# One transformer layer on one core: where two norm weights and the attention gates are multiplied in

## The chip, the cores and the metric

The kernel runs on one core of a Trainium2 chip. The metric is device time in microseconds for one execution; lower is better. The kernel before takes 1735.78 us, the median of three runs (1735.76 to 1736.35).

The engines are named as the profile names them: PE is TensorE (matrix products; PEld are its weight loads), DVE is VectorE, ACT is ScalarE, POOL is GpSimd, and SP is the engine whose queue issues the DMAs. A line number such as L207 is a line of the kernel before.

## The reference, cut to what matters

```python
def rms_norm(x, g):
    xf = x.astype(jnp.float32)
    y = xf * lax.rsqrt(jnp.mean(xf * xf, axis=-1, keepdims=True) + RMS_EPS)
    return (y * g.astype(jnp.float32)).astype(x.dtype)

def hybrid_layer(x, mem, norm_mix, w_in, ...):
    xn = rms_norm(x, norm_mix)              # 1024 rows of 1024 channels
    proj = xn @ w_in                        # q, k, v, gates, conv input, memory q, merge gates
    ...
    kvm = rms_norm(mem, norm_mem) @ w_mem_kv   # 256 rows of 1024 channels
    ...
    # nsa_attention, for each of three branches (compressed, selected, window):
    #   p = masked_softmax(s, mask); o = p @ v
    return gg[..., 0:1] * o_c + gg[..., 1:2] * o_s + gg[..., 2:3] * o_w
```

The rows of x and mem are divided by their root mean square and multiplied by one weight per channel. In the attention each head's probabilities are divided by their row sum, and each branch is multiplied by a sigmoid gate, one per row, head and branch.

## The kernel before

Products are made with operands split into a high part (rounded to a TensorE format) and a low part (the rest): `split(hi, lo, src)` is a copy on ACT (L131) and a subtraction on DVE (L128), and a product is three matmuls, all recorded at L144.

**Start.** x is read in four pairs of 128-row tiles (`rows2`, L229). For each pair `norm_x` calls `norm_pair`: for each of the two tiles a Square with a running sum on ACT (L205), a square root on ACT (L136), a reciprocal on DVE (L138), and a DVE operation (L207) that multiplies the tile by the row factor and by `gmix`, the norm weights spread over all 128 partitions, into a work slab. `gmix` is made by two products of a column of ones with the weight row (L324) and two DVE operations (L325). Then `transpose_pair` turns the pair with 16 PE transposes (L216) into four PSUM banks of 128 x 2 x 256, and each bank is split into a slab of `XN`. The first projection (memory queries, `raw_proj`, 48 matmuls of 128x256 per pair) follows each pair, and the convolution's input products follow that.

**Memory.** `norm_pair` also serves mem; its weights come in by a DMA that spreads them over the partitions (`gain_row`, L197).

**Attention.** Units (query tile, group, branch, head pair) run four ahead of their value products. `scores` makes the scores on PE, a masked minimum on DVE (L707, L679), the exponential with its sum on ACT (L711, L681), and ends in `softmax_tail`: a reciprocal of the sums (L645), a product with the gates into `c` (L651), both on DVE, and one POOL operation per head that multiplies the probabilities by `c` (L653). POOL also makes `qd`, the next query tile's queries times their norm weight (L661), which PE turns at L665.

**Order.** A scheduler sets each engine's order from the written program and its pools of buffers; an engine then runs its list in order. Products of the merge gates (`pf` banks, `fsl` weights) are written with a lower priority as filler, so that they stand wherever other PE work is not ready; from the thirteenth on their weights' subtraction is on POOL (L128).

Of the kernel before, what the change touches and what calls it, by code (L numbers as in the profile page):

```python
# [8 lines left out]
F32 = mybir.dt.float32  # L9
F32R = mybir.dt.float32r  # L10
BF16 = mybir.dt.bfloat16
# [6 lines left out]
P = 128  # L18
# [21 lines left out]
def hybrid_layer_kernel(  # L40
# [154 lines left out]
    def gain_row(src):  # L195
        g = t4([D])
        nc.sync.dma_start(g, src.to_broadcast([P, D]))  # L197
        return g

    def norm_pair(src, gain, dests, js):  # L200

        for tt in range(2):
            j = js[tt]
            ss = small(1)
            nc.scalar.activation(j, src[:, tt, :], AF.Square, accum_out=ss)  # L205
            r = recip_rms(ss, D, RMS_EPS, 1)
            nc.vector.scalar_tensor_tensor(j, src[:, tt, :], r, gain, op0=OP.mult, op1=OP.mult)  # L207
        transpose_pair(js, dests)

    def transpose_pair(js, dests):  # L210
        for kp in range(4):
            b = bank([2, 256])
            for kk in range(2):
                k = 2 * kp + kk
                for tt in range(2):
                    nc.tensor.transpose(b[:, kk, tt * P:(tt + 1) * P], js[tt][:, k * P:(k + 1) * P], ident)  # L216
            hi, lo = dests(kp)
            split(hi, lo, b)
# [13 lines left out]
    def work2():  # L232
        js = slab([2, D], F32)
        return js[:, 0, :], js[:, 1, :]

    def norm_x(tp):
        half, q = tp // 2, tp % 2
        js = work2()
        if q == 0:
            for kp in range(4):  # L240
                XN[half][kp] = slab([2, 2, 512])
        norm_pair(xin[tp], gmix, lambda kp: tuple(XN[half][kp][:, hl, :, q * 256:(q + 1) * 256] for hl in range(2)),
                  js)
# [73 lines left out]
    xin = [rows2(x, 0)]  # L317
    g1 = [t2([512], p=1) for _ in range(2)]
    for half in range(2):
        nc.sync.dma_start(g1[half], norm_mix[:, half * 512:(half + 1) * 512])  # L320
    gmix = t4([D])
    for half in range(2):
        b = bank([512])
        nc.tensor.matmul(b, ones[0:1, :], g1[half], start=True, stop=True)  # L324
        nc.vector.tensor_scalar(gmix[:, half * 512:(half + 1) * 512], b, 512.0, None, op0=OP.mult)  # L325
# [138 lines left out]
    gme = gain_row(norm_mem)  # L464
    js = work2()
    MN = [slab([2, 4, 256]) for _ in range(2)]
    norm_pair(xs, gme, lambda kp: tuple(MN[kp // 2][:, hl, 2 * (kp % 2):2 * (kp % 2) + 2, :] for hl in range(2)), js)
# [174 lines left out]
    def softmax_tail(i, g, br, h0, den, tiles):  # L642
        n = len(tiles)
        rec, c = small(n), small(n)
        nc.vector.reciprocal(rec, den)  # L645
        c0 = (4 * g + h0) * 3 + br
        gate = gsb[:, i, c0:c0 + 3 * n - 2:3]
        if br == 0 and i == 0:
            nc.vector.scalar_tensor_tensor(c, rec, rowok, gate, op0=OP.mult, op1=OP.mult)
        else:  # L650
            nc.vector.tensor_tensor(c, rec, gate, op=OP.mult)  # L651
        for h in range(n):
            nc.gpsimd.tensor_scalar(tiles[h], tiles[h], c[:, h:h + 1], 1.0, op0=OP.mult, op1=OP.mult)  # L653
# [225 lines left out]
    def norm_h(tp):  # L879
# [14 lines left out]
        def turned(kp):  # L894
            b = bank([2, 256])
            for kk in range(2):
                k = 2 * kp + kk
                for tt in range(2):
                    nc.tensor.transpose(b[:, kk, tt * P:(tt + 1) * P], js[tt][:, k * P:(k + 1) * P], ident)
            split(XN[half][kp][:, 0, :, c], XN[half][kp][:, 1, :, c], b)  # L900
            return b
# [274 lines left out]
```

## Time and profile before

| what | us |
|---|---|
| median of three runs | 1735.78 |
| the profiled execution | 1737.04 |
| its span, first to last instruction | 1735.3 |
| PE busy in the span | 1704.0 |
| DVE busy | 1087.8 |
| ACT busy | 732.3 |
| POOL busy | 482.8 |

The rows further down are of four kinds. The page gives each engine's busy time. Tables by stretch give busy time in a window of the span, with the granted TensorE clock as a share of its full 2.4 GHz. Timelines list instructions in order of time; square brackets give the idle time just before and what ended it. Groups by form give count, busy time and mean duration of one kind of instruction.

### The profile page before, as it was taken

The numbers are of one execution on the slowest core, as the hardware profiler recorded it, in microseconds if no ns is written. First come the engines' busy times: TensorE is split into PE (matmuls) and PEld (weight loads), VectorE is DVE, ScalarE is ACT, GpSimd is POOL, SyncE is SP. The second block draws the span as 40 slices with busy tenths as digits, with TensorE's granted clock in tenths as the row PEclk, the third lists the DMA queues.
The fourth block names the chain that finished last, engine by engine and source line by source line (L and its number), as shares of the span: only waits on it lengthen the run. The fifth ranks groups of instructions, "written<-read, shape, count | busy, mean of one in ns | idle before, by whom it ended". The sixth has DMA issues, their size and how long they took to land. (4 is left out here: it accounts for less than half of the span.)

```text
span 1735.3 us, 25240 instructions
## 1 busy us (share of the span) xinstructions
PE 1704.0 (98%) x9483; PEld 1480.1 (85%) x9483; DVE 1087.8 (63%) x1885; ACT 732.3 (42%) x1378; POOL 482.8 (28%) x469
## 2 busy tenths in 40 slices
PE   6999999999999999999999999999999999999999
PEld 5887998999888889989888899788888888888887
DVE  5499897877345667777754624865544545457665
ACT  5211443344356666666653423632232322234332
POOL 0000001110134443444204500165556677410000
PEclk9999999999999999999999999999999999999999
DMA  6112442122111111111385322143233445794673
GB/s 203 47 38 97 135 121 90 39 73 74 49 61 56 56 49 34 31 46 50 106 306 183 109 80 98 73 134 98 91 122 97 158 149 167 256 388 153 223 240 122
DMA packets 178388, 204.08 MB, mean 118 GB/s; under 512 B 10774, under 2 KB 125750, under 8 KB 177242
## 3 DMA queue, kind: packets, MB, share of 16 engines
q1 hardware_dynamic: 178266, 202.47, 35.5%
q8 instruction: 74, 1.21, 0.3%
q14 instruction: 48, 0.39, 0.1%
HBM read 152.10 MB, written 50.33 MB: 117 GB/s over the span
## 5 line engine op out<-in xcount | busy, mean ns | idle before, releaser
L144 PE MATMUL ps<-slab,wsl 128*128 128x512 f32 (+1 forms) x1664 | 371.8, 382 | 3.0 <-DVE t L128 2.4
L144 PEld LDWEIGHTS ps<-slab,wsl 128*128 128x128 f32 x1664 | 303.1, 189 | 64.2 <-issue 2.6
L144 PE MATMUL pf<-slab,fsl 128*128 128x512 f32 x1236 | 321.5, 399 | 1.2 <-ACT fz L791 1.1
L144 PEld LDWEIGHTS pf<-slab,fsl 128*128 128x128 f32 x1236 | 223.3, 189 | 42.2 <-ACT fz L791 2.3
L144 PE MATMUL ps<-wsl,slab 128*128 128x256 f32 x1680 | 217.3, 285 | 0.0
L144 PEld LDWEIGHTS ps<-wsl,slab 128*128 128x128 f32 x1680 | 209.1, 193 | 2.0 <-issue 0.7
L1006 DVE TENSOR_TENSOR t<-ps,t 128x512 f32<-128x512 f32 x127 | 86.9, 688 | 113.9 <-PE ps L144 111.0
L365 DVE SCALAR_TENSOR_TENSOR slab<-slab,cw 128x1023 f32<-128x1023 f32 (+15 forms) x120 | 151.4, 1266 | 1.8
L144 PE MATMUL ps<-slab,fsl 128*128 128x512 f32 x636 | 147.7, 389 | 0.0
L144 PEld LDWEIGHTS ps<-slab,fsl 128*128 128x128 f32 x636 | 119.4, 188 | 24.8
L128 DVE TENSOR_TENSOR t<-ps,t 128x512 fp32r<-128x512 f32 (+3 forms) x196 | 120.3, 630 | 15.5 <-ACT t L131 14.0
L1110 PE MATMUL ps<-wsl 128*128 128x512 f32 x495 | 118.5, 389 | 0.0
L128 DVE TENSOR_TENSOR wsl<-st,wsl 128x1024 fp32r<-128x1024 f32 x65 | 84.7, 1303 | 53.5 <-ACT wsl L131 50.4
L144 PE MATMUL ps<-t,slab 128*128 128x256 f32 x624 | 115.5, 293 | 1.6 <-DVE t L128 1.0
L131 ACT CAST t<-ps 128x512 fp32r<-128x512 f32 (+2 forms) x192 | 98.0, 539 | 36.4 <-PE ps L739 25.4
L1110 PEld LDWEIGHTS ps<-wsl 128*128 128x128 f32 x495 | 92.9, 188 | 19.3
L131 ACT CAST wsl<-st 128x1024 fp32r<-128x1024 f32 x65 | 68.3, 1051 | 84.7 <-PE ps L144 45.4
L521 POOL TENSOR_SCALAR t<-t,sm 128x256 f32<-128x256 f32 x32 | 22.5, 722 | 288.1 <-DVE sm L517 288.1
L144 PEld LDWEIGHTS ps<-t,slab 128*128 128x128 f32 x624 | 94.9, 191 | 7.8 <-DVE t L128 1.7
L144 PE MATMUL ps<-slab,qt 128*128 128x384 f32 (+3 forms) x384 | 96.1, 342 | 1.9 <-DVE sm L707 1.9
L131 ACT CAST wsl<-t 128x1024 fp32r<-128x1024 f32 x42 | 44.3, 1054 | 97.8 <-POOL t L128 38.9
L1110 PE MATMUL ps<-fsl 128*128 128x512 f32 x330 | 79.8, 389 | 0.0
(233 smaller groups left out, 2693.6 us busy)
## 6 DMA issues: line engine op xcount, KB each, us to landing
t<-in_w_down_dram SPq DMA_DIRECT2D x70, 256.0 KB, 4.3
fst<-in_w_in_dram SPq DMA_DIRECT2D x24, 512.0 KB, 3.8
zd<-fz SPq DMA_DIRECT2D x48, 256.0 KB, 2.0
t<-zd SPq DMA_DIRECT2D x24, 512.0 KB, 4.1
st<-in_w_in_dram SPq DMA_DIRECT2D x22, 512.0 KB, 4.0
st<-in_w_gate_dram SPq DMA_DIRECT2D x22, 512.0 KB, 4.3
st<-in_w_up_dram SPq DMA_DIRECT2D x22, 512.0 KB, 4.1
ad<-t SPq DMA_DIRECT2D x44, 256.0 KB, 2.4
```

The source lines that it names most:

```text
L128: eng.tensor_tensor(o, a, b, op=OP.subtract)
L131: nc.scalar.copy(hi, src)
L144: m = nc.tensor.matmul(o, a, b, start=start, stop=stop)
L365: return nc.vector.scalar_tensor_tensor(acc[:, s:], u[:, :S - s], cw[:, ct, 30 - s:31 - s], acc[:, s:], op0=OP.mult, op1=OP.add)
L521: nc.gpsimd.tensor_scalar(pm[:, tt, h, :], pm[:, tt, h, :], rec[:, j:j + 1], 1.0, op0=OP.mult, op1=OP.mult)
L1006: nc.vector.tensor_tensor(o, a_, b_, op=OP.add)
L1110: nc.tensor.matmul(B[t], a_, b_, start=start and k == 0 and j == 0, stop=k == FH - 1 and j == 2, skip_group_check=True)
```

## The change

`gain_row`, `work2` and the weight products are gone. The weights of both norms come in as 16 rows of 128 numbers, are turned once on PE, and stay as `gcol`, a tile of 128 x 16 with one weight per partition. `norm_pair` scales the rows in place with the row factor alone (a DVE operation with one scalar), and turns them from there. After the turn a channel lies on a partition, so the weight is applied in the split: per bank two ACT copies of 128x256 with a scale from `gcol` and two DVE operations of 128x256, where one of each on 128x512 stood. The second tile of the first pair is read after the weight rows. The Square writes to a small BF16 tile.

In `softmax_tail` the product `c` is gone: POOL multiplies by the reciprocal and by the gate at once. In the first query tile's compressed branch a DVE operation multiplies the reciprocal by `rowok`.

```diff
-    def norm_pair(src, gain, dests, js):
+    gcol = const([2 * KT], F32, "gcol")
+    def norm_pair(src, g0, dests):
         for tt in range(2):
-            j = js[tt]
+            v = src[:, tt, :]
             ss = small(1)
-            nc.scalar.activation(j, src[:, tt, :], AF.Square, accum_out=ss)
+            nc.scalar.activation(t2([D], BF16), v, AF.Square, accum_out=ss)
             r = recip_rms(ss, D, RMS_EPS, 1)
-            nc.vector.scalar_tensor_tensor(j, src[:, tt, :], r, gain, op0=OP.mult, op1=OP.mult)
-        transpose_pair(js, dests)
+            nc.vector.tensor_scalar(v, v, r, None, op0=OP.mult)
+        for kp in range(4):
+            b = turned_pair([src[:, tt, :] for tt in range(2)], kp)
+            hi, lo = dests(kp)
+            for kk in range(2):
+                g = gcol[:, g0 + 2 * kp + kk:g0 + 2 * kp + kk + 1]
+                nc.scalar.activation(hi[:, kk], b[:, kk], AF.Copy, scale=g)
+                nc.vector.scalar_tensor_tensor(lo[:, kk], b[:, kk], g, hi[:, kk].bitcast(F32), op0=OP.mult,
+                                               op1=OP.subtract)
...
-    xin = [rows2(x, 0)]
-    g1 = [t2([512], p=1) for _ in range(2)]
-    for half in range(2):
-        nc.sync.dma_start(g1[half], norm_mix[:, half * 512:(half + 1) * 512])
-    gmix = t4([D])
-    for half in range(2):
-        b = bank([512])
-        nc.tensor.matmul(b, ones[0:1, :], g1[half], start=True, stop=True)
-        nc.vector.tensor_scalar(gmix[:, half * 512:(half + 1) * 512], b, 512.0, None, op0=OP.mult)
+    xin = [slab([2, D], F32)]
+    nc.sync.dma_start(xin[0][:, 0, :], x[:P, :])
+    rows = t2([P], p=2 * KT)
+    nc.sync.dma_start(rows[:KT, :], norm_mix.rearrange("o (k p) -> (o k) p", p=P))
+    nc.sync.dma_start(rows[KT:, :], norm_mem.rearrange("o (k p) -> (o k) p", p=P))
+    nc.sync.dma_start(xin[0][:, 1, :], x[P:2 * P, :])
+    b = bank([2 * KT])
+    nc.tensor.transpose(b, rows, ident[:2 * KT, :2 * KT])
+    nc.vector.tensor_copy(gcol, b)
...
     def softmax_tail(i, g, br, h0, den, tiles):
         n = len(tiles)
-        rec, c = small(n), small(n)
+        rec = small(n)
         nc.vector.reciprocal(rec, den)
-        c0 = (4 * g + h0) * 3 + br
-        gate = gsb[:, i, c0:c0 + 3 * n - 2:3]
         if br == 0 and i == 0:
-            nc.vector.scalar_tensor_tensor(c, rec, rowok, gate, op0=OP.mult, op1=OP.mult)
-        else:
-            nc.vector.tensor_tensor(c, rec, gate, op=OP.mult)
+            nc.vector.tensor_scalar(rec, rec, rowok, None, op0=OP.mult)
         for h in range(n):
-            nc.gpsimd.tensor_scalar(tiles[h], tiles[h], c[:, h:h + 1], 1.0, op0=OP.mult, op1=OP.mult)
+            c0 = (4 * g + h0 + h) * 3 + br
+            nc.gpsimd.tensor_scalar(tiles[h], tiles[h], rec[:, h:h + 1], gsb[:, i, c0:c0 + 1], op0=OP.mult, op1=OP.mult)
```

ACT at the start, before: after the first tile's Square (L205) come the casts of the first two weight units (`st` to `wsl`), and the first pair's four banks are split before the second pair's Square.

```order
L205 ACTIVATE slab_173,sm_178<-slab_139 128x1024
L131 CAST wsl_155<-st_153 128x1024
L136 ACTIVATE sm_180<-sm_178 128x1
L131 CAST wsl_160<-st_158 128x1024
L205 ACTIVATE slab_173,sm_185<-slab_139 128x1024
L136 ACTIVATE sm_187<-sm_185 128x1
L131 CAST slab_174<-ps_192 128x2x256
L131 CAST slab_175<-ps_199 128x2x256
L131 CAST slab_176<-ps_206 128x2x256
L131 CAST slab_177<-ps_213 128x2x256
L205 ACTIVATE slab_220,sm_221<-slab_163 128x1024
L136 ACTIVATE sm_223<-sm_221 128x1
```

ACT at the start, now (its lines are those of the changed kernel: L203 the Square, L136 the root, L211 the scaled copy of half a bank; `slab_140` is the first pair of x, `slab_159` the second):

```order
L203 ACTIVATE t_17_174,sm_173<-slab_140 128x1024
L136 ACTIVATE sm_176<-sm_173 128x1
L203 ACTIVATE t_21_182,sm_181<-slab_140 128x1024
L136 ACTIVATE sm_184<-sm_181 128x1
L131 CAST wsl_151<-st_149 128x1024
L131 CAST wsl_156<-st_154 128x1024
L211 ACTIVATE slab_169<-ps_189,gcol 128x256
L211 ACTIVATE slab_170<-ps_198,gcol 128x256
L203 ACTIVATE t_29_226,sm_225<-slab_159 128x1024
L211 ACTIVATE slab_171<-ps_207,gcol 128x256
L211 ACTIVATE slab_172<-ps_216,gcol 128x256
L136 ACTIVATE sm_228<-sm_225 128x1
```

Both Squares and roots of the first pair now stand ahead of the weight casts, and the second pair's Square stands between the first pair's half-bank copies.

DVE at the start, before, from the first weight unit's subtraction on (`slab_174` to `slab_177` are the first pair's split slabs):

```order
L128 TENSOR_TENSOR wsl_155<-st_153,wsl_155 128x1024
L138 RECIPROCAL sm_182<-sm_180 128x1
L325 TENSOR_SCALAR t_5_146<-ps_150 128x512
L128 TENSOR_TENSOR wsl_160<-st_158,wsl_160 128x1024
L207 SCALAR_TENSOR_TENSOR slab_173<-slab_139,sm_182,t_5_146 128x1024
L138 RECIPROCAL sm_189<-sm_187 128x1
L207 SCALAR_TENSOR_TENSOR slab_173<-slab_139,sm_189,t_5_146 128x1024
L128 TENSOR_TENSOR slab_174<-ps_192,slab_174 128x2x256
```

DVE at the start, now (L205 is the scaling in place, L212 the low half of a bank):

```order
L138 RECIPROCAL sm_186<-sm_184 128x1
L205 TENSOR_SCALAR slab_140<-slab_140,sm_186 128x1024
L128 TENSOR_TENSOR wsl_151<-st_149,wsl_151 128x1024
L128 TENSOR_TENSOR wsl_156<-st_154,wsl_156 128x1024
L212 SCALAR_TENSOR_TENSOR slab_169<-ps_189,gcol,slab_169 128x256
L212 SCALAR_TENSOR_TENSOR slab_170<-ps_198,gcol,slab_170 128x256
L212 SCALAR_TENSOR_TENSOR slab_171<-ps_207,gcol,slab_171 128x256
L212 SCALAR_TENSOR_TENSOR slab_172<-ps_216,gcol,slab_172 128x256
L138 RECIPROCAL sm_230<-sm_228 128x1
L212 SCALAR_TENSOR_TENSOR slab_169<-ps_189,gcol,slab_169 128x256
L205 TENSOR_SCALAR slab_159<-slab_159,sm_230 128x1024
```

The scaling of the first pair has moved ahead of the weight subtractions, and the second pair's first scaling stands among the first pair's half banks. On PE nothing moves at this place: the 16 transposes of the first pair and four of the second still stand ahead of the first projection matmul.

DVE in the attention, fifth query tile, before (`sm_5357` is `c`; L707 is the masked minimum of the next unit):

```order
L645 RECIPROCAL sm_5356<-sm_5337 128x2
L651 TENSOR_TENSOR sm_5357<-sm_5356,gsb 128x2
L707 ISA wsl_5392,sm_5393<-ps_5395,strip 128x384
L707 ISA sm_5393 128x1
L128 TENSOR_TENSOR t_963_5457<-ps_5456,t_963_5457 128x512
```

DVE at the same place, now (L640 is the reciprocal, L699 the masked minimum):

```order
L640 RECIPROCAL sm_5313<-sm_5294 128x2
L699 ISA wsl_5347,sm_5348<-ps_5350,strip 128x384
L699 ISA sm_5348 128x1
L128 TENSOR_TENSOR t_919_5408<-ps_5407,t_919_5408 128x512
L699 ISA wsl_5347,sm_5348<-ps_5354,strip,sm_5348 128x256
```

The product with the gates is gone from between the reciprocal and the next masked minimum.

## Rows read from the trace of the kernel before

**Rows 1.** The page, busy time of each engine and share of span.

```profile
PE 1704.0 (98%) x9483; PEld 1480.1 (85%) x9483; DVE 1087.8 (63%) x1885; ACT 732.3 (42%) x1378; POOL 482.8 (28%) x469
```

**Rows 2.** By stretch: length, busy PE, PEld, DVE, ACT, POOL; clock; DMA share, GB/s.

```profile
0.00:30.00 30.00, 16.50 (x83) 13.14 (x84) 16.87 (x24) 15.91 (x27) 3.13 (x13) 0.94 0.85 275
30.00:60.00 30.00, 28.60 (x212) 26.94 (x212) 14.64 (x23) 13.83 (x29) 0.26 (x2) 1.00 0.10 30
...
600.00:700.00 100.00, 97.79 (x618) 88.29 (x619) 67.78 (x228) 62.38 (x151) 40.09 (x53) 0.98 0.13 40
...
1200.00:1300.00 100.00, 100.00 (x443) 82.81 (x442) 49.11 (x57) 28.69 (x37) 56.80 (x38) 1.00 0.35 111
```

**Rows 3.** Timeline of the start: start us, us, engine, line, instruction, idle before.

```profile
4.46 1.06 ACT L205 ACTIVATE slab<-slab 128x1024 f32<-128x1024 f32 x1 [2.17 <-DMA slab<-in_x_dram]
...
8.12 1.04 ACT L131 CAST wsl<-st 128x1024 fp32r<-128x1024 f32 x1 [2.50 <-DMA st<-in_w_in_dram]
...
9.53 1.04 ACT L131 CAST wsl<-st 128x1024 fp32r<-128x1024 f32 x1 [0.27 <-DMA st<-in_w_in_dram]
...
11.00 1.22 DVE L128 TENSOR_TENSOR wsl<-st,wsl 128x1024 fp32r<-128x1024 f32 x1
...
12.13 1.28 DVE L207 SCALAR_TENSOR_TENSOR slab<-slab,sm,t 128x1024 f32<-128x1024 f32 x1
...
15.80 2.51 ACT L131 CAST slab<-ps 128x512 fp32r<-128x512 f32 x4 [3.93 <-PE ps L216]
16.41 2.61 DVE L128 TENSOR_TENSOR slab<-ps,slab 128x512 fp32r<-128x512 f32 x4 [1.61 <-ACT slab L131]
18.20 1.06 ACT L205 ACTIVATE slab<-slab 128x1024 f32<-128x1024 f32 x1
...
19.49 1.04 ACT L205 ACTIVATE slab<-slab 128x1024 f32<-128x1024 f32 x1
...
21.16 1.12 PE L216 MATMUL ps<-ident,slab 128*128 128x128 f32 x4 [3.48 <-DVE slab L207]
...
21.92 4.82 PE L144 MATMUL ps<-wsl,slab 128*128 128x256 f32 x29
...
44.71 0.63 PE L216 MATMUL ps<-ident,slab 128*128 128x128 f32 x4 [1.40 <-DVE slab L207]
```

**Rows 4.** PE alone by stretch of 2 us: length, busy PE, granted clock, DMA share.

```profile
22.00:24.00 2.00, 2.00 (x12) 0.50 0.40 102
...
650.00:652.00 2.00, 2.00 (x8) 0.50 0.00 0
```

**Rows 5.** Groups by form: count, busy us, mean ns of one, idle before.

```profile
L128 DVE TENSOR_TENSOR t<-ps,t 128x256 fp32r<-128x256 f32 x40 | 16.4, 417 | 1.2 <-ACT t L131 1.1
...
L364 DVE TENSOR_SCALAR slab<-slab,cw 128x1024 f32<-128x1024 f32 x4 | 3.2, 809 | 0.0
...
L515 ACT ACTIVATE t<-ps,sm 128x256 f32<-128x256 f32 x32 | 14.8, 473 | 31.9 <-DVE sm L511 31.8
...
L131 ACT CAST slab<-ps 128x256 fp32r<-128x256 f32 x8 | 3.0, 370 | 5.8 <-DVE t L290 5.8
```

**Rows 6.** Timeline of the attention around 645 us.

```profile
641.73 2.41 POOL L128 TENSOR_TENSOR fsl<-fst,fsl 128x1024 fp32r<-128x1024 f32 x1 [2.67 <-ACT fsl L131]
...
642.77 1.38 DVE L651 TENSOR_TENSOR sm<-sm,gsb 128x2 f32<-128x2 f32 x1
...
647.64 0.50 PE L144 MATMUL ps<-slab,qt 128*128 128x256 f32 x2 [1.34 <-DVE sm L707]
```

**Rows 7.** Groups by form in the attention.

```profile
L651 DVE TENSOR_TENSOR sm<-sm,gsb 128x2 f32<-128x2 f32 x64 | 20.7, 323 | 5.6
...
L661 POOL TENSOR_TENSOR t<-slab,gn 128x512 f32<-128x512 f32 x16 | 20.7, 1296 | 88.0 <-DVE sm L287 88.0
...
L653 POOL TENSOR_SCALAR wsl<-wsl,sm 128x512 f32<-128x512 f32 x12 | 8.2, 695 | 6.1 <-DVE sm L651 5.9
```

**Rows 8.** PE's waits in the span: us in total, times, longest.

```profile
PE ps L665 <- POOL t L661: 1.8, 2, 0.9
```

More of the change, by code (lines that the diff above doesn't have):

```diff
@@ L193, in hybrid_layer_kernel, with turned_pair @@
     md = drp.tile([4, P, S], F32, tag="md", name="md")
[L195 to L198, printed above, removed]
-    def norm_pair(src, gain, dests, js):
+    gcol = const([2 * KT], F32, "gcol")
+    def norm_pair(src, g0, dests):
         for tt in range(2):
-            j = js[tt]
+            v = src[:, tt, :]
             ss = small(1)
-            nc.scalar.activation(j, src[:, tt, :], AF.Square, accum_out=ss)
+            nc.scalar.activation(t2([D], BF16), v, AF.Square, accum_out=ss)
             r = recip_rms(ss, D, RMS_EPS, 1)
-            nc.vector.scalar_tensor_tensor(j, src[:, tt, :], r, gain, op0=OP.mult, op1=OP.mult)
-        transpose_pair(js, dests)
-    def transpose_pair(js, dests):
+            nc.vector.tensor_scalar(v, v, r, None, op0=OP.mult)
         for kp in range(4):
-            b = bank([2, 256])
+            b = turned_pair([src[:, tt, :] for tt in range(2)], kp)
+            hi, lo = dests(kp)
             for kk in range(2):
[L214 to L218, printed above, removed]
+                g = gcol[:, g0 + 2 * kp + kk:g0 + 2 * kp + kk + 1]
+                nc.scalar.activation(hi[:, kk], b[:, kk], AF.Copy, scale=g)
+                nc.vector.scalar_tensor_tensor(lo[:, kk], b[:, kk], g, hi[:, kk].bitcast(F32), op0=OP.mult,
+                                               op1=OP.subtract)
+    def turned_pair(js, kp):
+        b = bank([2, 256])
+        for kk in range(2):
+            k = 2 * kp + kk
+            for tt in range(2):
+                nc.tensor.transpose(b[:, kk, tt * P:(tt + 1) * P], js[tt][:, k * P:(k + 1) * P], ident)
+        return b
     XN = [[None] * 4 for _ in range(2)]
@@ L230, in rows2 @@
         return xs
-    def work2():
-        js = slab([2, D], F32)
-        return js[:, 0, :], js[:, 1, :]
     def norm_x(tp):
         half, q = tp // 2, tp % 2
-        js = work2()
         if q == 0:
@@ L241, in norm_x @@
                 XN[half][kp] = slab([2, 2, 512])
-        norm_pair(xin[tp], gmix, lambda kp: tuple(XN[half][kp][:, hl, :, q * 256:(q + 1) * 256] for hl in range(2)),
-                  js)
+        norm_pair(xin[tp], 0, lambda kp: tuple(XN[half][kp][:, hl, :, q * 256:(q + 1) * 256] for hl in range(2)))
     def unit(src, shape, alloc=wslab, eng=None, load=False):
@@ L463, in hybrid_layer_kernel @@
     xs = rows2(mem, 0)
-    gme = gain_row(norm_mem)
-    js = work2()
     MN = [slab([2, 4, 256]) for _ in range(2)]
-    norm_pair(xs, gme, lambda kp: tuple(MN[kp // 2][:, hl, 2 * (kp % 2):2 * (kp % 2) + 2, :] for hl in range(2)), js)
+    norm_pair(xs, KT, lambda kp: tuple(MN[kp // 2][:, hl, 2 * (kp % 2):2 * (kp % 2) + 2, :] for hl in range(2)))
     def mn(hl, k, half, a, b):
@@ L894, in turned @@
         def turned(kp):
[L895 to L899, printed above, removed]
+            b = turned_pair(js, kp)
             split(XN[half][kp][:, 0, :, c], XN[half][kp][:, 1, :, c], b)
```

## The prediction

> **What bounds the kernel now.** I read the page first. PE is busy for 1704.0 of 1735.3 us [rows 1], so only 31 us of the span can be won by work that isn't PE's, and the question for every part of the change is whether it touches one of the places where PE stands. The table by stretch finds them [rows 2]: 13.5 us of PE's idle time lie in the first 30 us and 1.4 us in the next 30; 2.2 us lie between 600 and 700, where the attention runs; between 1200 and 1300 PE has no idle time at all. DVE, ACT and POOL are below 70% in the attention stretch, so work taken from them there is worth nothing by itself, only through a wait of PE that it shortens.
>
> The timeline of the start [rows 3] is to be read as one chain. The first tile of x is there at 4.46. ACT squares it, and then waits for a weight unit: the cast at 8.12 stands ahead of the root in its list, idle 2.50 us for the DMA, and the second cast at 9.53 is again set by a DMA. So the root comes at 9, the scalings L207 run from 12.13, the splits on ACT end at 18.3 and on DVE at 19.0, and only behind them ACT takes the second pair's Squares (18.20 and 19.49). PE's first four transposes of the second pair (21.16, idle 3.48 us for L207) stand ahead of the first projection matmul, so real work begins at 21.92, with the clock at 0.50, that is 1.2 GHz, right after this idle time [rows 4].
>
> **The change at the start.** Three edits act on this chain. The Squares and roots of the first pair go ahead of the weight casts; the wait for `gmix` goes; the second pair's first Square goes between the first pair's half banks. Against them stands a dearer split. I walk the new lists with durations of the old trace.
>
> Prices. A half-bank copy on ACT with a scale from `gcol`: the plain 128x256 copy takes 0.37 us, and one of the same size with a per-partition operand (L515, an exponential) 0.47 [rows 5]; I take 0.47, since that operand is what is added, and keep 0.37 as the lower end. A half-bank low part on DVE: 0.42 for 128x256 from PSUM [rows 5], and L207, which has such an operand, takes 0.06 more than L128 of the same size (1.28 against 1.22) [rows 3]; I take 0.48, with ends 0.42 and 0.60. The scaling in place: L364 is the same kind of operation on the same size and takes 0.81 [rows 5]. A Square with its read takes 1.15, with the root 1.29, the step from 18.20 to 19.49 [rows 3].
>
> Walk. The first tile at 4.46 is squared, rooted and scaled by about 7; the second tile, issued two small DMAs later, lies between 4.46 and the next arrival at 8.12, so its scaling ends near 9 and at the latest near 10.5. The 16 transposes then end before or near 12. ACT is held by the second weight cast, which ends at 9.53 + 1.04 = 10.57 whatever else moves. From there its list is two halves (to 11.5), the Square of the second pair (to 12.7), two halves (13.1, 13.6), a root (13.8), and then the second halves (14.3, 14.7). DVE ends the second weight subtraction at 10.6 + 1.22 = 11.85, does two halves (12.8), two more as ACT delivers them (13.7, 14.2), a reciprocal (14.4), one half (14.9), and then the scaling of the second pair's first tile, which ends at 15.7. Now PE has its four transposes, at 15.75 where the old ones began at 21.16. The gain at that point is 5.4 us; with the cheaper prices 5.9, with the dearer 4.9. What follows on PE is the same as from 21.16 on, at the same half clock for its first microseconds, so nothing is taken back there.
>
> The Trainium skill, "VectorE: DVE Perf Modes", section "Mode 2×_2P — use both read ports for one tensor", says that a one-source fp32 operation in SBUF yields two results per cycle. My estimate from its 0.96 GHz is 0.53 us for 1024 elements, where row L364 shows 0.81; by the page the gain at the transposes would be 5.7 and the time 0.3 us lower. The row decides.
>
> Later in the start two waits trade places. The third pair's transposes need the banks of the second pair, whose second halves ACT reaches only after the four Squares and roots of pairs three and four (4 x 1.29), five half-bank copies (5 x 0.47) and two weight casts (2 x 1.04); that puts the release near 28.4, while PE, after 48 matmuls, 20 transposes and four filler matmuls, is there near 26.7. I charge 1.7 us. In return the wait of 1.40 us at 44.71 goes [rows 3], since by then all Squares are done. Net at the start: 5.4 - 1.7 + 1.4 = 5.1, I take **5.0 us**, ends 2.5 (the late bank waits twice) and 6.5. The filler matmuls that no longer stand in the first 60 us are only moved; PE does them later, and they cost nothing net. The two `gmix` products on PE lie in time when PE has nothing else, so their loss is worth nothing beyond the chain. The 512 KB read of mem's weights was far ahead of need, and mem's norm lies under PE work; both at nothing.
>
> **The change in the attention.** L651 is removed 64 times at 0.32 us on average, 20.7 us [rows 7] with the two-head form alone. One row shows why it is dear for two columns: at 642.77 it takes 1.38 us and ends when POOL's subtraction, begun at 641.73 for 2.41 us, ends [rows 6]. The masked minimum behind it is late, and PE waits 1.34 us at 647.64 for the bank that it frees. That is a PE wait, and it goes. Behind it the clock stood at 0.50 for all of the 2 us from 650 on [rows 4], which cost 1.0 us more. Together that is 2.3; I take **2.0 us** for the attention as a whole, with ends of 0, if another place of the remixed list waits instead, and 4.0. Everything else of the 20.7 us is DVE time under busy PE.
>
> The Trainium skill, "GPSIMD Engine Reference", section "Key points", says that POOL shares its SBUF interfaces with VectorE and contends with DVE instructions that have two SBUF inputs. The trace agrees at 642.77, and by the rule every such stall of L651 must go, since the reciprocal that is left has one input. That frees DVE time, but not more of PE's than the row at 647.64 bears out, so the sum by the rule is the same.
>
> POOL's scaling now reads two per-partition scalars. No row shows that form. Its price lies between 0 more (it reads one operand already and multiplies by 1.0) and that of a two-input operation: L661 takes 1.296 us for 128x512, L653 0.695 [rows 7], so up to 0.60 more per head. I take 0, being nearest to L653, which is the same operation with a constant in that place.
>
> Sum against the profiled span: 5.0 + 2.0 = 7.0 us, 1735.3 to 1728.3. The profiled execution was 1737.04 as a whole, the median is 1735.78; taking the same 7.0 off the median gives 1728.8 us.
>
> **The rivals.** *Only the start gains.* The attention's order is remixed over hundreds of places, and a new wait takes the place of the one at 647.64: 1735.8 - 5.0 = 1730.8. For it speaks that the 2.2 us of PE's idle time from 600 to 700 [rows 2] hold more than the one wait of 1.34, so other places are near to waiting too.
>
> *The split eats the start.* Per pair ACT does eight halves (3.8 us) where four copies took 2.5, and all 32 halves before the convolution products cost 5 us more. If ACT and not PE paces the second to fourth pair, that comes off the 5.4: 1735.8 - 0.4 - 1.5 = 1733.9. Against it: ACT is busy for 13.8 of the 30 us from 30 to 60 [rows 2], and in my walk the last halves are done some us before PE asks for them.
>
> *The scaling on POOL becomes late* (slower than before). If two scalars cost what two inputs do, each head takes up to 0.60 us longer; two heads stand in POOL's list ahead of each of the 16 `qd` operations, so each is 1.2 us later. PE already waits twice on it, 1.8 us [rows 8]. If all 16 places are uncovered, that is 19 us against the 7 gained: 1748. It decides from the sixth uncovered place on. Against it: POOL is at 40% [rows 2], and filler stands before most of these places.
>
> **How the numbers follow.** A difference of about 0.2%, 3.5 us, is what a measurement of this kernel can tell from no change; faster by more means below 1732.3. The forecast has 0.50, only the start 0.22, the eaten start 0.17, late POOL 0.07, and 0.04 is left for a loss of another kind. The first two are faster but for their upper ends, so faster 0.68; the third and those ends are the same, 0.22; the slower side has 0.10. The range goes from 1723.5 (both terms at their good ends and a little more) to 1735.0, which takes in the eaten start; above it lie the slower cases.
>
> **What would show it.** Right at the start: the first projection matmul between 16 and 17.5, the half-bank copies at 0.47 us, one wait of PE of 1 to 2 us near 27, and none near 44. In the attention: no DVE operation of two columns above 0.3 us, no wait of over 1 us at a score matmul around 640, POOL's scalings as long as before. Wrong would be the second tile of x landing after 8, a PE that waits for splits of each pair in turn, or scalings on POOL near 1.2 us for 128x512.

## The result and the profile after

The changed kernel takes 1725.63 us, the median of four runs (1724.24 to 1726.64), against 1736.07 before. The ratio is 0.9938, with a 95% interval of 0.9921 to 0.9956: faster by 10.4 us where 7.0 were forecast. The profiled execution took 1726.1 us, its span is 1724.4, 10.9 less than before. The page's line of busy times, beside [rows 1]:

```profile
PE 1698.5 (98%) x9480; PEld 1479.9 (86%) x9480; DVE 1065.0 (62%) x1826; ACT 732.9 (42%) x1396; POOL 498.0 (29%) x469
```

PE is busy for 5.5 us less, and its idle time falls from 31.3 to 25.9, 5.4 less. Of the 5.5 us, 3.75 are the two `gmix` products, which filled idle time of the start. The other 1.7 are not a drop of the clock: the traces record three before (near 22, 650 and 1097 us) and two now (near 286 and 1084), but the start ran at the slower pace in both kernels (last section). PE stops nine times less often (32 stretches of work become 23), and in the traces the last matmul before a stop counts with some 0.18 us more than one in a row; my estimate from this is 9 x 0.18 = 1.6 us. The table by stretch says where the idle time changed. First of the kernel after (length, busy PE, PEld, DVE, ACT, POOL, granted clock, DMA share, GB/s), in three of the stretches of [rows 2] and three more:

```profile
0.00:30.00 30.00, 18.14 (x113) 16.70 (x114) 20.55 (x44) 24.30 (x53) 3.40 (x15) 1.00 0.86 270
30.00:60.00 30.00, 30.00 (x211) 27.75 (x210) 16.59 (x31) 12.67 (x24) 0.00 (x0) 1.00 0.24 62
600.00:700.00 100.00, 99.18 (x649) 90.37 (x649) 66.97 (x227) 68.14 (x163) 45.82 (x54) 1.00 0.13 41
...
180.00:200.00 20.00, 18.00 (x108) 15.39 (x107) 17.36 (x28) 14.09 (x30) 0.00 (x0) 1.00 0.42 132
280.00:320.00 40.00, 36.90 (x201) 30.96 (x200) 24.73 (x33) 13.89 (x23) 3.77 (x4) 0.96 0.32 99
480.00:860.00 380.00, 377.91 (x2381) 339.17 (x2380) 239.57 (x780) 245.51 (x603) 166.75 (x206) 1.00 0.18 57
```

The same three additional stretches of the kernel before:

```profile
180.00:200.00 20.00, 19.71 (x150) 18.45 (x149) 20.00 (x23) 12.48 (x25) 0.00 (x0) 1.00 0.64 219
280.00:320.00 40.00, 39.05 (x223) 33.26 (x222) 28.99 (x39) 16.45 (x31) 3.77 (x4) 1.00 0.34 106
480.00:860.00 380.00, 372.40 (x2328) 332.15 (x2327) 255.01 (x852) 240.58 (x598) 152.20 (x208) 1.00 0.16 51
```

Length less busy PE is idle time. It falls in the first 60 us (14.9 to 11.9) and, most of all, in the attention from 480 to 860 us (7.6 to 2.1). It rises at two places that the prediction does not name: 180 to 200 (0.3 to 2.0) and 280 to 320 (1.0 to 3.1).

**The start.** The timeline of the kernel after (start us, us, engine, line, instruction, idle before), to be laid beside [rows 3]; L203 is the Square, L211 and L212 are the halves of a split, L205 is the scaling in place, L220 the transposes:

```profile
7.54 1.06 ACT L203 ACTIVATE t<-slab 128x1024 bf16<-128x1024 f32 x1 [1.69 <-DMA slab<-in_x_dram]
...
9.10 1.05 ACT L131 CAST wsl<-st 128x1024 fp32r<-128x1024 f32 x1 [0.18 <-DMA st<-in_w_in_dram]
...
10.78 1.04 ACT L131 CAST wsl<-st 128x1024 fp32r<-128x1024 f32 x1 [0.63 <-DMA st<-in_w_in_dram]
...
11.73 0.83 ACT L211 ACTIVATE slab<-ps,gcol 128x256 fp32r<-128x256 f32 x2
...
15.24 0.74 DVE L205 TENSOR_SCALAR slab<-slab,sm 128x1024 f32<-128x1024 f32 x1
...
16.04 1.12 PE L220 MATMUL ps<-ident,slab 128*128 128x128 f32 x4 [3.26 <-DVE slab L205]
...
16.81 4.43 PE L144 MATMUL ps<-wsl,slab 128*128 128x256 f32 x25
```

The list is the one that the prediction walked. The second tile of x lands at 7.54 and the weights about 1 us later than before (9.10 and 10.78 against 8.12 and 9.53), so the second pair's first transposes come at 16.04, not 15.75, and the first projection matmul at 16.81 instead of 21.92. The convolution's first input product comes at 49.59 instead of 59.63; the filler ahead of it is 3.34 us shorter (4.44 us of it against 7.78), so the start gains 10.04 - 3.34 = 6.7 us, which agrees with 3.0 us less idle time and 3.75 us of `gmix` products.

**The new waits.** PE's waits of the kernel after between 60 and 480 us (total us, times, longest):

```profile
PE ps L526 <- POOL t L516: 1.8, 2, 1.0
PE ps L445 <- DVE t L128: 1.7, 1, 1.7
PE pf L144 <- ACT fz L783: 1.5, 3, 0.7
```

L445 turns the compressed keys at 186 us; its operand is the end of a short chain on DVE that stands between convolution taps. L526 turns the memory branch's probabilities at 283 us, which POOL scales (L516). The kernel before had a wait of 0.3 us on the first and none on the second.

At the second place DVE holds POOL up. Two of the four scalings, at 281.25 and 283.13, take 1.44 us, the other two 0.48. Each of the long ones runs beside a weight subtraction of DVE with two inputs (128x1024, begun at 281.04 and 282.81) and ends 0.35 us behind it. The kernel before has the same 3.77 us for the four. What differs is the filler that PE has in hand meanwhile, first in the changed kernel, then in the kernel before:

```profile
280.80 3.77 POOL L516 TENSOR_SCALAR t<-t,sm 128x256 f32<-128x256 f32 x4 [9.65 <-DVE sm L512]
281.83 0.48 PE L144 MATMUL pf<-slab,fsl 128*128 128x512 f32 x1
...
283.71 3.77 POOL L521 TENSOR_SCALAR t<-t,sm 128x256 f32<-128x256 f32 x4 [10.86 <-DVE sm L517]
284.06 2.77 PE L144 MATMUL pf<-slab,fsl 128*128 128x512 f32 x11
```

PE alone around this place (length, busy PE, clock, DMA share, GB/s):

```profile
282.00:284.00 2.00, 0.86 (x5) 1.00 0.26 36
284.00:286.00 2.00, 1.38 (x9) 0.93 1.00 346
286.00:288.00 2.00, 2.00 (x6) 0.50 0.88 264
288.00:290.00 2.00, 2.00 (x8) 0.72 0.05 18
```

Behind the idle time the clock goes to 0.50, 1.2 GHz, as it did at 650 in the kernel before [rows 4]. So the two places take back 3.9 us of idle time, and a drop of the clock of some 1.7 us (from the rows: 2 x (0.07 + 0.50 + 0.28)) comes here in the place of the one at 650, which is gone.

**The attention.** PE's waits between 480 and 860 us, first of the kernel before, then of the one after:

```profile
PE ps L144 <- DVE t L128: 2.1, 4, 1.0
PE ps L144 <- DVE sm L707: 1.9, 3, 1.3
PE ps L665 <- POOL t L661: 1.8, 2, 0.9
PE ps L739 <- DVE t L128: 0.8, 2, 0.5
```

```profile
PE ps L144 <- DVE t L128: 1.2, 2, 0.9
PE ps L657 <- POOL t L653: 0.5, 1, 0.5
PE ps L144 <- DVE sm L699: 0.2, 1, 0.2
```

Not one wait but all kinds of them shrink: those on the masked minimum, on the splits and on POOL's `qd`. What is placed so far sums to 6.7 - 3.9 + 5.5 = 8.3 us; with 0.4 us less idle time from 320 to 480 and 0.5 from 1080 to 1130 it is 9.2 of the 10.9. The other 1.7 are the busy time above.

### The profile page after: what moved, and what is told of

Read it like the earlier page. It is cut to its first block, busy times and chain, and to the rows that moved or that the text cites. A ratio compares the mean times of both kernels' runs of the same rounds, so it can differ in the third digit from the quotient of the medians.

```text
span 1724.4 us, 25204 instructions
## 1 busy us (share of the span) xinstructions
PE 1698.5 (98%) x9480; PEld 1479.9 (86%) x9480; DVE 1065.0 (62%) x1826; ACT 732.9 (42%) x1396; POOL 498.0 (29%) x469
## 4 chain that ended last, share of the span: by engine, by line
PE 94%; DVE 3%; ACT 1%; issue 1%; POOL 1%; DMA 0%; SPq 0%; ACTq 0%; DVEq 0%; POOLq 0%
PE ps L144 57%; PE pf L144 19%; PE ps L1098 11%; PE ps L731 3%; PE pf L1098 1%; DVE slab L362 1%; PE ps L220 1%; DMA st<-in_w_in_dram 0%; DVE t L128 0%; PE ps L657 0%; PE ps L715 0%; PE ps L526 0%; DVE slab L128 0%; DVE slab L417 0%; DVE slab L414 0%
## 5 line engine op out<-in xcount | busy, mean ns | idle before, releaser
L516 POOL TENSOR_SCALAR t<-t,sm 128x256 f32<-128x256 f32 x32 | 21.6, 695 | 312.1 <-DVE sm L512 312.1
L645 POOL TENSOR_SCALAR wsl<-wsl,sm,gsb 128x640 f32<-128x640 f32 (+7 forms) x76 | 60.0, 801 | 81.9 <-DVE sm L640 73.1
```

What stands on the lines that cost most here:

```text
L516: nc.gpsimd.tensor_scalar(pm[:, tt, h, :], pm[:, tt, h, :], rec[:, j:j + 1], 1.0, op0=OP.mult, op1=OP.mult)
L645: nc.gpsimd.tensor_scalar(tiles[h], tiles[h], rec[:, h:h + 1], gsb[:, i, c0:c0 + 1], op0=OP.mult, op1=OP.mult)
```

## Experiments

Times are medians; each is set against the kernel before on the same chip (1736.94 us in the first group of four, 1736.29 in the second, 1736.76 in the third). "Idle" is PE's.

**One part alone.** `e1_norm_only` is the changed kernel with the old `softmax_tail`, `e2_gates_only` the kernel before with the new one.

> The norms as in the changed kernel, the attention's gates as before (the product c on DVE, one scalar on POOL). If the two parts add up, the start keeps its gain: first projection matmul near 16.8 us, and 5 to 7 us below before, that is 1729 to 1731. The stretch from 480 to 860 us should again hold 5 to 8 us of PE's idle time, against 7.6 before and 2.1 in the changed kernel. Rival, order luck: the idle time there is low (under 4 us) although the product is back, and the time is near 1726.

> The norms as before, the gates as in the changed kernel. If the two parts add up: first projection matmul near 21.9 us, PE's idle time from 480 to 860 us about 2 us instead of 7.6, time 4 to 7 us below before, 1729 to 1732. Rival, order luck: idle time there above 5 us and a time within 2 us of before.

| | time | ratio, 95% | idle 0-60 | 180-200 | 280-320 | 480-860 |
|---|---|---|---|---|---|---|
| before | 1736.94 beside one part, 1736.07 beside both | | 14.9 | 0.3 | 1.0 | 7.6 |
| norm only | 1733.91 | 0.9986 (0.9978 to 0.9995) | 11.3 | 2.0 | 3.1 | 7.2 |
| gates only | 1728.46 | 0.9952 (0.9939 to 0.9964) | 15.2 | 0.3 | 1.0 | 2.1 |
| both | 1725.63 | 0.9938 (0.9921 to 0.9956) | 11.9 | 2.0 | 3.1 | 2.1 |

The stretches add up: each part changes its own, and the two new waits belong to the norm part. Alone it gains 3.0 us, the gates 8.5. The norm part misses the 1729 to 1731 that I expected, because the new waits come with it: 6.7 - 3.9 is 2.8. Its gain is just clear of the noise: three of its eleven executions took 1736.7 to 1737.7 us, the others 1732.4 to 1734.0.

**A dead product.** Is it the product's stall beside POOL, or its place in the chain from the sums to the scaled probabilities? `e3_dead_product` puts it back into the changed kernel, but nobody reads what it writes:

```diff
         nc.vector.reciprocal(rec, den)
+        d0 = (4 * g + h0) * 3 + br
+        nc.vector.tensor_tensor(small(n), rec, gsb[:, i, d0:d0 + 3 * n - 2:3], op=OP.mult)
```

> The changed kernel with the old DVE product of reciprocal and gates put back at its place behind each reciprocal; its result is used by nobody, so POOL does not wait for it. It is work added, nothing is left out. Theory A (the product's two SBUF inputs make DVE wait for POOL, and PE for DVE): some ten of the products take over 0.7 us, PE's idle time from 480 to 860 us rises from 2.1 to 5 us or more, and the time rises by 3 to 6 us, to 1729 to 1732. Theory B (the product only lengthened the chain from sum to scaled probabilities): no change, 1725 to 1727. Theory C (order luck): the idle time moves, but not with the long products.

1731.53 us (0.9969, 0.9958 to 0.9979); idle from 480 to 860 is 5.5 us. Timeline of this kernel at the place of [rows 6]:

```profile
639.97 2.40 POOL L128 TENSOR_TENSOR fsl<-fst,fsl 128x1024 fp32r<-128x1024 f32 x1 [2.79 <-ACT fsl L131]
...
640.74 0.17 DVE L640 RECIPROCAL sm<-sm 128x2 f32<-128x2 f32 x1 [1.65 <-ACT slab L705]
...
641.00 1.38 DVE L642 TENSOR_TENSOR sm<-sm,gsb 128x2 f32<-128x2 f32 x1
```

Beside the same POOL subtraction the reciprocal takes 0.17 us and the product 1.38; both the product and the subtraction end at 642.4. Seven dead products take over 0.7 us, fewer than the ten I expected; in the kernel before it was eleven, and each of these ended within 0.03 us of the end of a POOL subtraction. With nobody reading it, the dead product still brings back 3.4 of the 5.5 us of idle time, so most of the cost lies in DVE standing still, with what is queued behind it, and not in the chain.

**One input.** `e4_one_input` puts a multiplication by 1.0 with a single tensor input into the chain:

```diff
-        rec = small(n)
-        nc.vector.reciprocal(rec, den)
+        raw_, rec = small(n), small(n)
+        nc.vector.reciprocal(raw_, den)
+        nc.vector.tensor_scalar(rec, raw_, 1.0, None, op0=OP.mult)
```

> The changed kernel with one more DVE operation in the chain: the reciprocal times 1.0, two to four columns with one SBUF input, and POOL scales by its result and the gate. It has the length and the place of the old product without its second input. Theory A (two inputs): no operation above 0.3 us, PE's idle time from 480 to 860 us stays near 2 us, time 1725 to 1727. Theory B (chain): idle time and time rise as much as the old product cost, to 1729 to 1732.

1733.31 us (0.9977, 0.9968 to 0.9985), idle 5.8 us. What I expected was wrong in its premise. The line's view of the new operation (ns: min, median, max):

```profile
L641 DVE TENSOR_SCALAR sm<-sm x76: 157/169/1593, 481.2 to 851.7; 128x2 f32<-128x2 f32 x61, 128x4 f32<-128x4 f32 x15
```

An operation with one input stalls just as the product did: nine times over 0.7 us, up to 1.59. The Trainium skill, "GPSIMD Engine Reference", section "Key points", names DVE instructions in a 2-port perf mode beside those with two SBUF inputs; the prediction had used only the second half of that rule. That this operation runs in such a mode no row shows. So this run is no test of the chain, and another was needed.

**A longer chain that does not stall.** `e9_long_chain` uses three reciprocals in a row.

```diff
-        nc.vector.reciprocal(rec, den)
+        nc.vector.reciprocal(r1, den)
+        nc.vector.reciprocal(r2, r1)
+        nc.vector.reciprocal(rec, r2)
```

> The changed kernel, with the one reciprocal ahead of the scaling replaced by three in a row (1/(1/(1/x))), so that the chain from the row sums to the scaled probabilities is longer by two DVE operations on 2 to 4 columns, of a kind that took 0.15 to 0.18 us each and was never held up in either trace. Theory A (what the removed product cost was its stall beside POOL's two-input subtractions, not its place in the chain): PE's idle time between 480 and 860 us stays at 2.1 to 2.8 us and the time at 1725 to 1727.5 us. Theory B (the chain's length is what counted): idle 5 us or more there and 1729 us or more.

The second and third reciprocal, by line, and the stretch from 480 to 860 us:

```profile
L641 DVE RECIPROCAL sm<-sm x76: 165/166/181, 480.8 to 844.6; 128x2 f32<-128x2 f32 x61, 128x4 f32<-128x4 f32 x15
L642 DVE RECIPROCAL sm<-sm x76: 156/166/178, 481.0 to 844.8; 128x2 f32<-128x2 f32 x61, 128x4 f32<-128x4 f32 x15
```

```profile
480.00:860.00 380.00, 377.75 (x2377) 338.39 (x2376) 259.97 (x934) 246.44 (x606) 167.40 (x208) 1.00 0.18 56
```

Idle time there is 2.2 us, as in the changed kernel (2.1), with two operations more in the chain. The median, 1728.31 (1725.82 to 1729.22), lies 0.8 us above what the theory of the stall allowed and below what the theory of the chain asked; the attention accounts for none of that, and I leave it open.

**The partner away.** `e10_filler_dve` is the kernel before, product and all, with the filler weights' subtraction always on DVE:

```diff
-                         eng=nc.vector if n_ < N_EARLY else nc.gpsimd)
+                         eng=nc.vector)
```

> The kernel before, with the filler weights' subtraction on DVE for all 24 units instead of 12 on DVE and 12 on POOL; the gate product stays. Theory A: with no 2.4 us subtraction on POOL beside it, the product on DVE (L651) never takes over 0.35 us (before: 11 times 0.7 to 1.7 us); PE's idle time between 480 and 860 us falls from 7.6 to 2 to 3.5 us, and the time to 1728 to 1731.5 us, as where the product was taken out. DVE then does 12 times 1.2 us more, beside its slack. Theory B (the stall has nothing to do with the subtraction): idle stays at 6.5 us or more and the time at 1734.5 to 1737 us.

The product L651 in this kernel, where [rows 7] shows the mean of 323 ns before:

```profile
L651 DVE TENSOR_TENSOR sm<-sm,gsb x75: 149/161/166, 480.9 to 847.2; 128x2 f32<-128x2 f32 x61, 128x4 f32<-128x4 f32 x14
```

It never takes over 0.166 us (before: 11 times 0.7 to 1.7). Idle falls from 7.6 to 3.9 us, a little above the 2 to 3.5 expected, though DVE does twelve operations of about 1.35 us more. The clock drop at 650 is gone. The time is 1729.07 us (0.9959, 0.9946 to 0.9971): this small edit gives 7.2 us, where the gates gave 8.5. Of these, 1.2 us are idle time between 1080 and 1130 us, away from the products.

**The loads' order.** `e5_x_first` loads both tiles of the first pair ahead of the norm weights.

```diff
     nc.sync.dma_start(xin[0][:, 0, :], x[:P, :])
+    nc.sync.dma_start(xin[0][:, 1, :], x[P:2 * P, :])
     rows = t2([P], p=2 * KT)
...
-    nc.sync.dma_start(xin[0][:, 1, :], x[P:2 * P, :])
```

> The changed kernel, with both halves of the first input pair loaded ahead of the two loads of the norms' weights (in the changed kernel the second half comes behind them, and the Square of it waited for its data until 7.54 us). Theory A (the loads' order costs a microsecond): the second Square starts by 6.6 us, the first projection matmul at 15.7 to 16.2 us instead of 16.81, and the time is 0.3 to 1.2 us under the changed kernel's. Theory B (PE's start is set by the weights' loads and the halves of the split): first projection matmul at 16.6 us or later, no difference.

The second Square starts at 5.69 and the first projection matmul at 15.73; idle before 60 us falls by 1.1 to 10.8. The median is 1725.99 us (0.9939, 0.9926 to 0.9951): the microsecond at the start does not show in the time, in which executions of this kernel differ by 2.6 us among themselves.

**The split's price.** `e6_plain_split` splits whole banks and leaves out both norms' weights.

```diff
-            for kk in range(2):
-                g = gcol[:, g0 + 2 * kp + kk:g0 + 2 * kp + kk + 1]
-                nc.scalar.activation(hi[:, kk], b[:, kk], AF.Copy, scale=g)
-                nc.vector.scalar_tensor_tensor(lo[:, kk], b[:, kk], g, hi[:, kk].bitcast(F32), op0=OP.mult,
-                                               op1=OP.subtract)
+            split(hi, lo, b)
```

> The changed kernel with the transposed tiles split whole, without the norms' weights (it leaves out both weight vectors of the two norms): one ACT copy and one DVE subtraction on a whole bank in the place of two of each on halves. It prices the split. By the halves measured in the changed kernel (ACT 2 x 0.485, DVE 2 x 0.476 us against about 0.70 and 0.70 for a whole bank) each of the 16 splits before 30 us is 0.25 us shorter on either engine. If the split's length holds PE back at the start, the stretch from the first projection matmul (16.81 us) to 60 us has less idle and the time falls by 0.5 to 1.5 us; if PE's fillers hide it, idle before 60 us stays within 0.5 us of 11.9 and the time within 0.5 us of the changed kernel's, at 1725 to 1726.5 us, unless the order of the fillers changes again.

Idle before 60 us is 12.2 us, against 11.9 with the halves, and the first projection matmul comes at 17.20: the shorter split gains PE nothing at the start. It is no clean price, because the order changed there too: on DVE four whole banks (2.64 us) stand ahead of the second pair's scaling, which starts at 15.62, where five halves stood and it started at 15.24. The time is 1730.43 us (0.9964, 0.9952 to 0.9977), slower than with the halves, and the reason lies elsewhere, in another order. Its largest waits between 60 and 480 us:

```profile
PE ps L522 <- POOL t L512: 5.0, 4, 2.9
PE ps L144 <- DVE sm L695: 2.3, 1, 2.3
```

**What the order alone is worth.** `e7_before_turned` and `e8_after_turned` are the kernels before and after with the rotation of PSUM banks one bank on; no operation differs.

```diff
-    turn = [0, 0, 0]
+    turn = [0, 1, 0]
```

> The kernel before with the same shift of the PSUM bank rotation: the same operations, another order. Theory A (order alone moves a microsecond or more): idle between 60 and 480 us, 1.7 us in the kernel before, changes by over 1 us and the time by 1 to 4 us. Theory B (the kernel before has no waits there because its edit-free start leaves the producers early): idle stays under 2.2 us there and the time within 1 us of 1736.1.

> The changed kernel with the PSUM banks handed out in a rotation that starts one bank later: the same operations, another order of them. It measures what the order alone is worth. Theory A (the waits at 186 and 283 us are an accident of this order, not of the edit): they go or change by over 1 us, and the time moves by 1 to 4 us either way. Theory B (the edit itself makes these producers late): both waits stay within 0.5 us of 1.75 and 1.8 and the time within 1 us of 1725.6.

The kernel before goes to 1742.29 us (ratio 1.0032, 1.0021 to 1.0044): 5.5 us for nothing but order, more than the 1 to 4 expected, with idle between 60 and 480 us up from 1.6 to 6.4 and these waits, which it did not have:

```profile
PE ps L144 <- DVE slab L128: 3.2, 1, 3.2
PE pf L144 <- ACT fz L791: 3.1, 2, 2.4
```

The changed kernel stays at 1725.80 (0.9944, 0.9932 to 0.9957), but not because its waits are fixed: the one at 186 us on DVE is gone, the one on POOL's scaling grows from 1.8 to 3.0 us, and others come, 5.9 us of idle time against 5.1. The time alone would have hidden this. So waits of this size are a matter of the order, in either kernel, and of which producer happens to stand uncovered.

**Faster producers.** `e12_both_waits` scales half of the memory branch's probabilities on ACT and makes the compressed keys' low part on POOL.

```diff
-            split(cat[:, 0], cat[:, 1], kn)
+            split(cat[:, 0], cat[:, 1], kn, nc.gpsimd)
...
+                if h == 0:
+                    nc.scalar.mul(pm[:, tt, h, :], pm[:, tt, h, :], rec[:, j:j + 1])
+                    continue
```

> The changed kernel, with the memory branch's probabilities scaled half on ACT and half on POOL (all on POOL in the changed kernel), and the subtraction of the compressed keys' split (128x64) on POOL instead of DVE. Both are the producers that PE waits for in the new waits of the changed kernel at 186 us (1.75 us) and at 283 us (0.79 and 0.98 us), which also put the clock to its lower level at 284. Theory A (late producers cause these waits): both waits shrink to under 0.5 us, idle between 180 and 320 us falls from 5.1 to 2 us or less, no clock drop near 284, 1720.5 to 1723.5 us. Theory B (the order of the filler matmuls decides, and the new order leaves other waits): idle there stays at 4 us or more, 1724.5 to 1727 us.

It failed: 1730.57 us (0.9965, 0.9952 to 0.9977). Its waits between 60 and 480 us:

```profile
PE ps L144 <- DVE sm L702: 2.3, 1, 2.3
PE pf L144 <- ACT fz L786: 1.6, 2, 0.9
PE ps L144 <- ACT t L131: 1.5, 2, 1.0
PE ps L445 <- POOL t L128: 0.8, 1, 0.8
```

The wait on POOL's L516 is gone and that at L445 halved, but the scheduler made another order of it, with a wait of 2.3 us elsewhere and a drop of the clock behind it, at 462 us. So this run does not show that a faster producer is no cure, only that a gain at one place was lost to the order at others.

**Later use.** `e13_later_use` leaves the producers as they are (on top of `e5_x_first`) and writes the uses later, so that other matmuls stand between: the compressed keys are turned behind the second compression, and the memory attention's last product with the values stands behind the next function's first projection.

```diff
-    compress(0, *kin)
+    cat = compress(0, *kin)
     compress(1, *vin)
+    b = bank([P], F32R)
+    nc.tensor.transpose(b, cat.rearrange("p a d -> p (a d)"), identr)
+    nc.vector.tensor_copy(kcmp, b.bitcast(F32))
...
             pm[tp] = mem_softmax(hp, tp, QM[tp])
             raw_proj(ws, tp, dest)
+            if left:
+                mem_out(*left)
+            left = (hp, tp, pm[tp])
+        return left
...
     for tp in range(4):
         raw_proj(ws, tp, Q[1])
+        if tp == 0:
+            mem_out(*left)
```

> The kernel of the run with both halves of the first input pair first (changed kernel, idle 10.8 us before 60 us), with the use of late data put later in the program: the compressed keys' transpose comes behind the second compression, and each memory attention's last product with the values behind the next one's first projection. Theory A (the new waits at 186 and 283 us come from an order in which nothing lies between a late producer and PE): both waits go, idle between 180 and 320 us falls from 5.0 us to 1.5 or less, no clock drop there, and the time is 1719 to 1723 us. Theory B (what is gained at one place is given back at another, whatever the order): the waits move, idle from 60 to 480 us stays at 4 us or more and the time at 1724.5 us or more.

1717.76 us (1717.54 to 1717.83), ratio 0.9891 (0.9876 to 0.9906): 8.2 us under `e5_x_first`, 7.9 under the changed kernel, and below the 1719 to 1723 expected. The stretches with the old waits:

```profile
180.00:200.00 20.00, 18.84 (x110) 16.12 (x109) 14.75 (x24) 13.19 (x28) 0.00 (x0) 1.00 0.47 145
...
280.00:320.00 40.00, 39.91 (x292) 37.64 (x291) 31.83 (x45) 17.30 (x38) 5.76 (x9) 1.00 0.17 56
```

Idle in these two falls from 5.0 us in `e5_x_first` to 1.3, and the recorded clock stays at 1.00 up to 1076 us. In the whole span PE is idle for 21.1 us against 24.7 and busy for 1695.0 against 1698.1, 6.7 us in all. About 1.7 us of the busy time is the drop that `e5_x_first` had near 186. The other 1.4 go with fewer stops of PE (23 stretches of work become 16), about 1.3 us by the estimate above. Both waits went as the edit intended; how much of the 8.2 us is the luck of another order is not separated.

## Why the prediction was right, and where not

The time, the sign and the range were right, and the sum was nearly so because errors of its terms stood against each other; that part was luck.

**The start: 5.0 us forecast, 6.7 measured.** The walk held within 0.3 us up to the transposes. Its prices, in the groups by form of the kernel after, first 60 us (count, busy us, mean ns):

```profile
L212 DVE SCALAR_TENSOR_TENSOR slab<-ps,gcol,slab 128x256 fp32r<-128x256 f32 x32 | 13.5, 476 | 4.5 <-ACT slab L211 4.4
L211 ACT ACTIVATE slab<-ps,gcol 128x256 fp32r<-128x256 f32 x32 | 13.2, 485 | 0.8 <-DVE slab L212 0.7
...
L205 DVE TENSOR_SCALAR slab<-slab,sm 128x1024 f32<-128x1024 f32 x8 | 6.0, 753 | 0.2
```

They were taken as 0.48, 0.47 and 0.81. The scaling lies between the row it was taken from and the estimate from the Trainium skill ("VectorE: DVE Perf Modes", "Mode 2×_2P — use both read ports for one tensor"), 0.53, and nearer to the row. The step that failed is the late wait for the second pair's banks, 1.7 us near 27. The second pair's last half does end late, on DVE at 28.6, near the 28.4 of the walk. But PE, which was at the third pair's transposes at 25.13 and not 26.7, got banks for all sixteen of them without a wait, had ten filler matmuls among and behind them where the walk counted four, and did not stand once from 16.04 to 60 us. Without that charge the sum is 5.4 + 1.4 = 6.8. The wait at 44.71 is gone, as forecast.

**The attention: 2.0 us forecast, 8.5 alone.** The mechanism was right: the product stalls beside POOL's subtraction, and without it the masked minimum is early. `e10_filler_dve` shows this from the other side. The size was off because the term was read from one place, the only wait between 600 and 700 us that I had traced back. The stretch to look at was the whole attention: 7.6 us of idle time from 480 to 860 and eleven products over 0.7 us, each holding up all that is queued behind it on DVE. The clock term was small too: the row at 650 is the middle of a drop, and its neighbours (0.77 from 648 to 650, 0.88 from 652 to 654) make it 2 x (0.23 + 0.50 + 0.12) = 1.7 us, not 1.0. 5.5 us of the idle time went, and the clock drop at 650 with it; in `e2_gates_only` PE's busy time fell by 3.0 us too.

**What was not forecast: 3.9 us of idle time given back at 186 and 283, and a clock drop behind the second.** "A new wait takes the place of the old one" stood among the rivals, but in the attention; it came in stretches that the diff doesn't touch, through the order, which left late producers uncovered. At 283 the producer was late by the very contention that the prediction used at 642, the other way round. This is why the norm part alone gains 3.0 us and not 6.7.

**POOL's two scalars: 0 forecast, 0.08 us each.** The changed kernel's groups by form from 480 to 860 us:

```profile
L645 POOL TENSOR_SCALAR t<-t,sm,gsb 128x64 f32<-128x64 f32 x60 | 22.7, 397 | 64.6 <-DVE sm L640 57.8 <-ACT t L131 6.3 <-PE ps L731 0.5
...
L645 POOL TENSOR_SCALAR wsl<-wsl,sm,gsb 128x512 f32<-128x512 f32 x12 | 9.2, 776 | 5.1 <-DVE sm L640 5.1
```

Before, these took 0.321 and 0.695 us. The price does not grow with the width between 64 and 1024 columns, and is far from the 0.60 of the rival; `qd` is waited for less than before (0.5 us against 1.8 [rows 8]), so the slow side never opened. The eaten start was not seen either: PE's waits before 60 us are on the scaling (7.3 us) and on a DMA (4.6), and `e6_plain_split` gained nothing by a shorter split. In that rival's sum the 1.5 us beside the 0.4 come from no row; no run shows what they stand for.

## What to carry to other kernels

A two-column operation on DVE can cost what is left of the POOL operation beside it (here up to 1.69 of 2.4 us), and POOL can wait for DVE in the same way: look at the maximum of each small group, not its mean, and first ask whether its partner can move. When an edit changes a scheduler's order, read the idle time of every stretch afterwards, and measure once what order alone is worth (here up to 5.5 us); writing the use of a late producer later removed its wait and kept the gain, while faster producers shortened their waits and lost the gain to another order.

## What was not expected of the hardware

- A DVE operation with one FP32 input and output of two columns, all in SBUF, waits for POOL's two-input subtraction (2.4 us) to end, up to 1.59 us, just as one with two inputs does, while a reciprocal of the same two columns takes 0.15 to 0.18 us at the same moment. The Trainium skill, "SBUF — State Buffer", section "SBUF: two separate sides", says that the shared port pair is an exclusive lock held for a whole instruction; the ends at 642.4 in `e3_dead_product` agree. Why the reciprocal is free of it is not shown.
- The wait goes the other way too. POOL's scaling of 128x256 took 1.44 us in the place of 0.48 beside DVE's two-input subtraction at 281 and at 283, and one of 128x128 took 1.49 in the place of 0.45 at 487.70, beside one of 1.26 us.
- A second per-partition scalar costs POOL's scaling 0.08 us at 64 columns and at 512.
- A granted clock of 1.00 can be a missing record. [rows 4] shows 12 matmuls from 22 to 24 us at 0.50; in `e2_gates_only` the same stretch has 11, and shows 1.00 (length, busy PE, clock, DMA share, GB/s):

```profile
22.00:24.00 2.00, 2.00 (x11) 1.00 0.29 79
```

  The first clock record of that trace begins at 26.4 us, that of the changed kernel at 19.5. At just these times the matmuls go from 0.21 us apart to 0.12, as they do in the kernel before at 24.4, where its recorded 0.50 ends. So the first projection matmuls of the changed kernel, 25 in 4.43 us, ran at the pace of 1.2 GHz up to 19.5 us, and the 1.00 of its first 30 us is no measurement before that.
- A stop of 2 us need not be followed by a drop: from 180 to 200 us PE was idle for 2.00 us in the changed kernel, at a granted clock of 1.00, and for 1.92 in `e5_x_first`, at 0.91. What decides it is open. One drop costs about 1.7 us, so differences of that size between two traces may be a drop and not the edit.
